# Moving the elementwise work between two layers from GpSimd to VectorE, and exchanging the places of three expert ranks

## The chip, the cores and the metric

The kernel runs on one core of a Trainium2 chip. The core has TensorE (PE in the profile; its weight loads are PEld), VectorE (DVE), ScalarE (ACT), GpSimd (POOL) and SyncE (SP), which here only issues loads. The metric is the device time of one execution in microseconds (us), median of several runs. The profile is that of one execution, and its times count from the start of its span.

## The reference, cut to what matters

Two layers work on 256 latent tokens and 256 context tokens of width 1024. Layer 0 is a recurrent block, layer 1 is attention with 16 query heads and 4 key heads. Behind each stands a mixture of 16 experts, of which every token takes two:

```python
for e in range(N_EXPERTS):
    y = y + gates[..., e:e + 1] * ((silu(h @ w1[e]) * (h @ w3[e])) @ w2[e])
ctx = ctx + cg_f * y[:, :C]          # layer 0: gain of the context
x = x + g_f * y[:, C:]               # layer 0: gain of the latent tokens
hx = modulate(x, ...); hc = modulate(ctx, ...)     # RMS norm, scale, shift
qx, kx, vx = split(hx @ qkv_w); kc, vc = split(hc @ qkv_w[:, q_cols:])
```

The stretch that the change works on is the end of layer 0's experts, the sum, the norm, and the projections of keys, values and queries.

## The kernel before, in words

**Experts of layer 0.** The 16 experts run in 16 slots, one after the other (`run`, lines 1166 to 1224). Slots 0 to 2 hold experts 0 to 2. The others are sorted by their number of tokens (rank 0 has the most), and `ORDERS` (line 38) says which rank stands in which slot: its 13 entries are slots 3 to 15. `ROOM` (line 39) gives each rank its rows: 192, 128, four times 96 (ranks 2 to 5), six times 64 (ranks 6 to 11), 32 (rank 12). `AGAIN` (line 41) lists the ranks that also have a second block of 128 rows under a run-time condition (rank 6 among them); such a slot costs branches on the engines in `ups`, `downs` and `fetch_next`, and its lists have two parts.

Each slot adds its result to the buffer `yr` in HBM by scatters that GpSimd issues (line 992), with accumulation. Each waits until the one before it has landed. A room of 64 or 32 rows takes one scatter, a room of 96 takes two (`BLOCKS`, line 63: a part of 64 rows and one of 32). Before the change the last three slots hold ranks 6, 5 and 12: one scatter, two, one. The weights of the experts are loaded by SP in a fixed order, 6 MB for each slot, into a ring of buffers.

**Between the experts and the attention** (`enter`, from line 1311). Weights and activations are split in two parts, `hi` (rounded) and `lo = w - hi`, and a product is three matmuls (`mm3`, line 180). The steps, in order of the code:

- `parts` (line 1337) splits one of the eight pieces of a weight: ScalarE copies to `hi`, and the engine given as `low` subtracts (line 1341). For the keys' and values' weights (`wkv`, line 1344) VectorE and GpSimd take turns; for the queries' weights (`wq`, line 1425) it is always GpSimd.
- `yr` is read back in four chunks of 128 tokens (line 1371), in the order 2, 3, 0, 1. Chunks 2 and 3 are latent tokens, 0 and 1 context.
- `gain(a)` (line 1377) multiplies a chunk with its gain: on VectorE for chunks 2 and 3, on GpSimd for 0 and 1. `add(a)` (line 1380) adds it to the residual on VectorE, and ScalarE squares and sums it. `modulated(a)` (line 1387) scales by the reciprocal root.
- `turn(a)` (line 1394) transposes a chunk on TensorE. For each of two halves it scales and shifts (VectorE for half 0, ScalarE for half 1, lines 1409 and 1407), rounds to `hhi` (VectorE, line 1411) and subtracts to `hlo` (line 1412): on VectorE for half 0, on GpSimd for half 1.
- `project_kv(a)` (line 1414) is a chunk's product with `wkv`; `project(n)` (line 1422) a half of the queries, with the splits of its weights; `keys` (line 1467), `norms` and `queries` are the norm and the rotation, on VectorE and ScalarE.

The block of lines 1509 to 1521 holds its own instructions in the written order on each engine, but the compiler's list scheduler may set instructions from outside it, such as the queries' splits, between them.

Of the kernel before, what the change touches and what calls it, by code (L numbers as in the profile page):

```python
# [34 lines left out]
ADA_AT = [32, 34]  # L35


ORDERS = [[11, 0, 10, 1, 9, 2, 8, 3, 7, 4, 6, 5, 12], [2, 0, 3, 1, 4, 5, 6, 7, 8, 9, 10, 11]]
ROOM = [[192, 128, 96, 96, 96, 96, 64, 64, 64, 64, 64, 64, 32], [160, 160, 32] + 9 * [32]]

AGAIN = [[1, 2, 3, 4, 6], [2, 3]]
# [25 lines left out]
def base(i, k):  # L67

    return BASE if k < FIRST[i] else ROOM[i][ORDERS[i][k - FIRST[i]]]


def again(i, k):

    return k < FIRST[i] or ORDERS[i][k - FIRST[i]] in AGAIN[i]


def room(i, k):
    return base(i, k) + 128 * again(i, k)
# [9 lines left out]
def hybrid_kernel(ctx: ExitStack, tc: tile.TileContext, x, c, ctxt, c_ctx, ada_w, ada_b, norm_mix_w, norm_ffn_w,  # L88
# [3 lines left out]
    nc = tc.nc  # L92
# [12 lines left out]
    def bank(name="bank"):  # L105
        if "spare" in banks:
            return banks["spare"]()
        return banks["pool"].tile([128, 512], F32, tag="bank", name=name)
# [61 lines left out]
    def take(key):  # L170
        return live[key][0]
# [394 lines left out]
    with tc.tile_pool(reuse_waits="tile", name="big0", bufs=1) as bp:  # L566
# [3 lines left out]
        hlo = hp.tile([128, NK, 512], F32R, name="hlo")  # L570
# [25 lines left out]
        with tc.tile_pool(reuse_waits="tile", name="n0", bufs=2) as n0, \  # L596
# [8 lines left out]
            hhi = wp.tile([128, 4096], F32R, tag="w", name="hhi").rearrange("p (k t) -> p k t", k=NK)  # L605
            parts = wp.tile([128, 4096], F32R, tag="w", name="parts")
# [704 lines left out]
    def enter(yr):  # L1311
# [6 lines left out]
        hlo = px.tile([128, 4096], F32R, tag="w", name="hlo1").rearrange("p (k t) -> p k t", k=NK)  # L1318
# [6 lines left out]
        def wide(name, dt=F32R):  # L1325
            return spare(name, dt).rearrange("p (k f) -> p k f", k=NK)

        wkv, wkvl, hhi = wide("wkv"), wide("wkvl"), wide("hhi")
        misc = spare("misc", F32)
        qd = [misc[:, 2048 + 1024 * z:3072 + 1024 * z].rearrange("p (h b f) -> p h b f", h=8, b=2) for z in range(2)]  # L1330
        gf = [misc[:, 2048 + 1024 * z:3072 + 1024 * z] for z in range(2)]
        n1 = ExitStack()
        yp = n1.enter_context(tc.tile_pool(reuse_waits="tile", name="n1", bufs=1))
        ys = [misc[:, 1024 * z:1024 * z + 1024] for z in range(2)] + [yp.tile([128, D], F32, name=f"y{z}") for z in (2, 3)]
        A, B = scale_vec(1, SC_M, 96, "am1"), vec(1, SH_M)

        def parts(key, hi, lo, k, low):

            w = take(key).rearrange("p (k f) -> p k f", k=NK)[:, k, :]
            nc.scalar.activation(hi[:, k, :], w, AF.Copy)  # L1340
            low.tensor_sub(lo[:, k, :], w, hi[:, k, :])

        for k in range(NK):
            parts(("qkv", 2), wkv, wkvl, k, (nc.vector, nc.gpsimd)[k % 2])
        region.close()
        pinned.__exit__(None, None, None)
        with tc.manual_schedule(engines={ET.PE, ET.Activation, ET.DVE, ET.Pool}):
# [27 lines left out]
        wq, wql = wide("wq"), wide("wql")  # L1375

        def gain(a):
            (nc.gpsimd, nc.vector)[a // 2].tensor_mul(ys[a], ys[a], gf[a // 2])

        def add(a):  # L1380
            nc.vector.tensor_add(xr[:, a, :], xr[:, a, :], ys[a])
            junk = ap.tile([128, D], BF16, tag="rtmp", name="junk", bufs=1)
            ss[a] = ap.tile([128, 1], F32, tag="ss", name="ss", bufs=4)
            nc.scalar.activation(junk, xr[:, a, :], AF.Square, accum_out=ss[a])
            nc.scalar.activation(ss[a], ss[a], AF.Sqrt, bias=eps, scale=1.0 / D)

        def modulated(a):
            nc.vector.reciprocal(ss[a], ss[a])
            if a < 2:
                nc.scalar.activation(ys[a], xr[:, a, :], AF.Copy, scale=ss[a])  # L1390
            else:
                nc.vector.tensor_scalar(ys[a], xr[:, a, :], ss[a], None, ALU.mult)

        def turn(a):
            j, ts = a // 2, slice(a * 128, a * 128 + 128)
            pbs = [bank(), bank()]
            for h in range(2):
                for k in range(4):
                    nc.tensor.transpose(pbs[h][:, k * 128:(k + 1) * 128], ys[a][:, (4 * h + k) * 128:(4 * h + k + 1) * 128],
                                        ident)  # L1400
            for h in range(2):
                m = yp.tile([128, 4, 128], F32, tag="m", name="m", bufs=2)
                for k in range(4):
                    kk = 4 * h + k
                    src = pbs[h][:, k * 128:(k + 1) * 128]
                    if h:
                        nc.scalar.activation(m[:, k, :], src, AF.Identity, bias=B[:, kk, j:j + 1], scale=A[:, kk, j:j + 1])
                    else:
                        nc.vector.tensor_scalar(m[:, k, :], src, A[:, kk, j:j + 1], B[:, kk, j:j + 1], ALU.mult, ALU.add)
                ks = slice(4 * h, 4 * h + 4)  # L1410
                nc.vector.tensor_copy(hhi[:, ks, ts], m)
                (nc.vector, nc.gpsimd)[h].tensor_sub(hlo[:, ks, ts], m, hhi[:, ks, ts])

        def project_kv(a, between=None):
            ts = slice(a * 128, a * 128 + 128)
            kvs[a] = pb = bank()
            for k in range(NK):
                if k == 4 and between is not None:
                    between()
                mm3(pb, hhi[:, k, ts], hlo[:, k, ts], wkv[:, k, :], wkvl[:, k, :], k == 0, k == NK - 1)  # L1420
# [88 lines left out]
        with tc.manual_schedule(engines={ET.PE, ET.Activation, ET.DVE, ET.Pool}):  # L1509
            gain(2)  # L1510
            add(2)
            gain(3)
            gain(0)
            gain(1)
            modulated(2)
            add(3)
            turn(2)
            modulated(3)
            project_kv(2, lambda: turn(3))
            for a in range(2):  # L1520
                add(a)
        project_kv(3)

# [13 lines left out]
        for a in range(2):  # L1537
            modulated(a)
            turn(a)
# [43 lines left out]
    class Heads:  # L1583
# [46 lines left out]
        def step(self, t):  # L1630
# [4 lines left out]
            if t >= 10 and t % 4 == 2:  # L1635
                self.weigh((t - 10) // 4)

    moe(R0, enter)
    with actx:
        heads = Heads()  # L1640
# [25 lines left out]
def _constants():  # L1666
# [30 lines left out]
    for i in range(2):  # L1697
        k = FIRST[i]
        a[:, C_KEY + 16 * i:C_KEY + 16 * i + 16] = np.where(x < k, 65536 + 16384 * (k - 1 - x), E - 1 - x)
        a[:, C_RANK + 16 * i:C_RANK + 16 * i + 16] = list(range(k)) + [k + r for r in ORDERS[i]]  # L1700
        a[:, C_ROOM + 16 * i:C_ROOM + 16 * i + 16] = [room(i, k) for k in range(E)]
# [32 lines left out]
```

## Time and profile before

| what | value |
|---|---|
| median of 3 runs | 992.27 us (991.25 to 992.55) |
| the profiled execution | 991.52 us, span 989.9 us |
| PE busy | 848.3 us (86% of the span) |
| DVE busy | 489.8 us (49%) |
| ACT busy | 302.8 us (31%) |
| POOL busy | 247.4 us (25%) |
| mean granted TensorE clock | 0.942 |

Shares over the whole span mix stages with different limits. Layer 0's experts run from about 317 to 595 us; the stretch from there to the first attention scores ends at about 675 us. In the timeline rows below the columns are start, duration (of a merged group of instructions), engine, line, operation, tiles, and in brackets how long the engine was idle before and what ended that. In rows of waits they are: the waiting engine, tile and line, what it waited for, us in total, times, the longest. In rows by source line: duration in ns (shortest, median, longest), first and last start.

### The profile page before, as it was taken

What the parts mean: (1) busy time and instruction counts of PE and PEld (TensorE: products, weight loads), DVE (VectorE), ACT (ScalarE), POOL (GpSimd) and SP (SyncE); (2) the same over time, 40 slices, a digit from 0 to 9 for tenths busy, and PEclk for the clock granted to TensorE, in tenths of its full rate; (3) what the DMA queues carried; (4) which work ended last, traced back from release to release, by engine and by line L of the source; (5) the groups of instructions that cost most, each with busy time, mean ns of one, the idle gap of its engine ahead of it and who ended that gap; (6) DMA issues with size and microseconds to landing.
All of it is one profiled execution on the core that took longest, in us unless ns stands there. A gap on an engine that the chain in (4) does not pass through costs nothing. (4 is left out here: it accounts for less than half of the span.)

```text
span 989.9 us, 17139 instructions
## 1 busy us (share of the span) xinstructions
PE 848.3 (86%) x6495; PEld 536.3 (54%) x6495; DVE 489.8 (49%) x1372; ACT 302.8 (31%) x555; POOL 247.4 (25%) x189
## 2 busy tenths in 40 slices
PE   3789899889996999999998963699999689799983
PEld 1356676575454655555555533487664555455652
DVE  2778797653147731312231115687861574523463
ACT  3546555674021211001010103556961220101110
POOL 2162233400002320211221115652430132312232
PEclk9899999998997999999999977799999799999997
DMA  9955974799525699999999994212939769999980
GB/s 346 358 183 200 388 262 170 259 386 383 205 83 214 215 360 384 371 356 362 355 342 365 376 338 133 102 58 77 388 125 393 272 234 373 376 388 361 376 270 10
DMA packets 126926, 277.11 MB, mean 280 GB/s; under 512 B 7673, under 2 KB 12889, under 8 KB 126816
## 3 DMA queue, kind: packets, MB, share of 16 engines
q1 hardware_dynamic: 116064, 253.77, 70.1%
q0 software_dynamic: 8880, 15.54, 6.7%
q10 hardware_dynamic: 1872, 6.37, 1.7%
q8 instruction: 64, 1.05, 0.4%
q14 instruction: 46, 0.38, 0.1%
HBM read 290.85 MB, written 14.81 MB: 309 GB/s over the span
## 5 line engine op out<-in xcount | busy, mean ns | idle before, releaser
L943 PE MATMUL up<-w,xg 128*64 128x256 f32 (+2 forms) x1888 | 173.8, 350 | 9.7 <-DMA w<-in_moe_w_dram 9.0
L943 PEld LDWEIGHTS up<-w,xg 128*64 128x64 f32 (+2 forms) x1888 | 108.6, 130 | 67.7 <-issue 32.2
L978 PE MATMUL py<-w,sx 128*32 128x256 f32 (+2 forms) x768 | 127.2, 513 | 5.9 <-DVE sx L957 4.0
L948 DVE TENSOR_TENSOR sx<-sx,up 128x256 f32<-128x256 f32 (+3 forms) x31 | 13.5, 434 | 186.5 <-PE up L943 108.9
L978 PEld LDWEIGHTS py<-w,sx 128*32 128x32 f32 (+2 forms) x768 | 44.8, 133 | 69.9 <-issue 52.8
L947 ACT ACTIVATE sx<-up 128x256 f32<-128x256 f32 (+3 forms) x31 | 12.2, 394 | 228.9 <-PE up L943 225.9
L582 POOL TENSOR_TENSOR parts<-w,parts 128x1024 fp32r<-128x1024 f32 x16 | 40.5, 2530 | 123.6 <-DVE parts L581 115.6
L992 POOL DMA_INDIRECT yr<-y,yi x21 | 32.8, 1564 | 122.0 <-DVE y L989 51.5
L528 PE MATMUL bank<-w,yT 128*128 128x512 f32 x128 | 57.3, 595 | 0.0
L182 PE MATMUL bank<-hhi,parts 128*128 128x512 f32 x128 | 52.3, 409 | 4.0 <-DVE parts L581 4.0
L184 PE MATMUL bank<-hhi,parts 128*128 128x512 f32 x128 | 51.5, 403 | 3.2 <-POOL parts L582 3.2
L183 PE MATMUL bank<-hlo,parts 128*128 128x512 f32 x128 | 52.3, 409 | 2.0 <-DVE hlo L397 1.9
L943 PE MATMUL up<-w,xr 128*32 128x128 f32 (+2 forms) x736 | 51.3, 315 | 2.9 <-issue 2.0
L915 POOL DMA_INDIRECT xg<-hr,gi x21 | 20.8, 990 | 124.0 <-DVE f L906 77.0
L316 PE MATMUL bank<-w,st 128*32 128x512 f32 x384 | 46.5, 615 | 3.5 <-DMA w<-in_ada_w_dram 3.1
L943 PEld LDWEIGHTS up<-w,xr 128*32 128x32 f32 (+2 forms) x736 | 35.5, 120 | 16.0 <-issue 10.5
L930 ACT ACTIVATE xg<-tp 128x512 f32<-128x512 f32 x32 | 17.4, 594 | 84.3 <-PE tp L925 71.8
L989 DVE TENSOR_SCALAR y<-py,gt 128x512 f32<-128x512 f32 (+1 forms) x21 | 14.4, 687 | 56.6 <-PE py L978 54.9
L462 DVE TENSOR_TENSOR rt<-bank,gm 128x512 f32<-128x512 f32 x12 | 8.3, 691 | 66.9 <-PE bank L528 66.9
L528 PEld LDWEIGHTS bank<-w,yT 128*128 128x128 f32 x128 | 23.4, 190 | 25.7 <-issue 25.5
L1607 POOL TENSOR_SCALAR pe<-pe,mx 128x512 f32<-128x512 f32 x16 | 25.0, 1567 | 45.3 <-DVE mx L1602 30.0
L992 POOL DMA_INDIRECT out_dram<-xr,yi x14 | 22.1, 1581 | 50.9 <-DVEq L1163 11.9
(358 smaller groups left out, 1624.6 us busy)
## 6 DMA issues: line engine op xcount, KB each, us to landing
w<-in_moe_w_dram SPq DMA_DIRECT2D x192, 1024.0 KB
w<-in_ada_w_dram SPq DMA_DIRECT2D x48, 1024.0 KB
w<-in_lru_in_w_dram SPq DMA_DIRECT2D x8, 1024.0 KB
w<-in_attn_qkv_w_dram SPq DMA_DIRECT2D x6, 1024.0 KB
w<-in_lru_out_w_dram SPq DMA_DIRECT2D x4, 1024.0 KB
w<-in_attn_o_w_dram SPq DMA_DIRECT2D x4, 1024.0 KB
hr<-h ACTq DMA_DIRECT2D x6, 512.0 KB
yr<-zero POOLq DMA_DIRECT2D x4, 512.0 KB
```

The costliest lines, as they stand in the source:

```text
L182: nc.tensor.matmul(pb, wh, xh, start=start, stop=False, skip_group_check=True)
L183: nc.tensor.matmul(pb, wh, xl, start=False, stop=False, skip_group_check=True)
L184: nc.tensor.matmul(pb, wl, xh, start=False, stop=stop, skip_group_check=True)
L316: nc.tensor.matmul(pa[32 * g:32 * g + 32, :], st[:, 4 * r + g, :], w[:, 4 * r + g, :], start=r == 0, stop=r == 1, skip_group_check=True, t ...
L528: nc.tensor.matmul(pb, src[:, k, n * 128:(n + 1) * 128], w[:, k, :], start=k == 0, stop=k == NK - 1)
L582: nc.gpsimd.tensor_sub(lo, w, h)
L915: nc.gpsimd.indirect_dma_start(out=dst[0:rows, :], out_offset=None, in_=hr[:, :], in_offset=bass.IndirectOffsetOnAxis(ap=idx[0:rows, :], a ...
L930: nc.scalar.activation(dst, pb, AF.Copy)
L943: nc.tensor.matmul(pw[g * Tn:(g + 1) * Tn, at:at + fg], hT[:, k, t0:t0 + Tn], W[:, k, g * fg:(g + 1) * fg], start=k == 0, stop=k == NK - 1 ...
L978: nc.tensor.matmul(py[j * Tn:(j + 1) * Tn, 0:wd], aT[:, ao + q * 128 + g * Tn:ao + q * 128 + (g + 1) * Tn], W2[:, f, j * dg + h * 512:j * ...
L992: nc.gpsimd.indirect_dma_start(out=yr[:, :].rearrange("r (g f) -> (r g) f", g=G), out_offset=bass.IndirectOffsetOnAxis(ap=ls.yi[:, z, b:b ...
L1607: (nc.gpsimd if u else nc.vector).tensor_scalar(pe, pe, mx[:, 1:2], None, ALU.mult)
```

## The change

The keys' and values' weights are split by VectorE alone; all four gains and all lower halves of the activations are computed by VectorE. The gains of chunks 0 and 1 now come right before their additions. GpSimd keeps its scatters, gathers and the queries' splits. In layer 0, slot 3 gets rank 6 (was 11), slot 13 rank 5 (was 6), slot 14 rank 11 (was 5).

```diff
-ORDERS = [[11, 0, 10, 1, 9, 2, 8, 3, 7, 4, 6, 5, 12], [2, 0, 3, 1, 4, 5, 6, 7, 8, 9, 10, 11]]
+ORDERS = [[6, 0, 10, 1, 9, 2, 8, 3, 7, 4, 5, 11, 12], [2, 0, 3, 1, 4, 5, 6, 7, 8, 9, 10, 11]]
...
         for k in range(NK):
-            parts(("qkv", 2), wkv, wkvl, k, (nc.vector, nc.gpsimd)[k % 2])
+            parts(("qkv", 2), wkv, wkvl, k, nc.vector)
...
         def gain(a):
-            (nc.gpsimd, nc.vector)[a // 2].tensor_mul(ys[a], ys[a], gf[a // 2])
+            nc.vector.tensor_mul(ys[a], ys[a], gf[a // 2])
...
                 nc.vector.tensor_copy(hhi[:, ks, ts], m)
-                (nc.vector, nc.gpsimd)[h].tensor_sub(hlo[:, ks, ts], m, hhi[:, ks, ts])
+                nc.vector.tensor_sub(hlo[:, ks, ts], m, hhi[:, ks, ts])
...
             gain(3)
-            gain(0)
-            gain(1)
             modulated(2)
...
             for a in range(2):
+                gain(a)
                 add(a)
```

## Rows read from the trace of the kernel before

**Rows 1.** Windows of three stretches: us, busy time by engine, PEclk, DMA share, GB/s
```profile
560.00:586.00 26.00, 18.83 (x257) 10.39 (x255) 2.21 (x5) 1.44 (x4) 3.10 (x2) 0.84 1.04 376
...
643.00:655.90 12.90, 12.90 (x66) 10.74 (x65) 10.20 (x23) 6.51 (x16) 5.62 (x4) 1.00 0.19 73
655.90:671.00 15.10, 13.89 (x69) 11.33 (x68) 13.46 (x29) 7.60 (x18) 8.22 (x7) 1.00 0.33 119
```

**Rows 2.** Waits from 596 to 672 us
```profile
PE bank L1399 <- DVE y L1392: 12.4, 1, 12.4
...
PE bank L184 <- POOL hlo L1412: 5.2, 1, 5.2
...
PE bank L1504 <- DVE misc L1498: 1.2, 1, 1.2
DVE m L1409 <- POOL hlo L1412: 1.2, 1, 1.2
```

**Rows 3.** Timeline of POOL from 561 to 640 us
```profile
561.50 1.55 POOL L992 DMA_INDIRECT yr<-y,yi  x1 [7.73 <-issue]
570.82 1.55 POOL L992 DMA_INDIRECT yr<-y,yi  x1 [7.77 <-DVEq L1163]
590.10 1.55 POOL L992 DMA_INDIRECT yr<-y,yi  x1 [17.73 <-DVE y L989]
596.99 1.55 POOL L992 DMA_INDIRECT yr<-y,yi  x1 [5.33 <-issue]
600.77 1.55 POOL L992 DMA_INDIRECT yr<-y,yi  x1 [2.23 <-DMA yr<-y,yi]
...
613.35 5.93 POOL L1378 TENSOR_TENSOR misc<-misc 128x1024 f32<-128x1024 f32 x2 [1.24 <-DMA misc<-yr]
...
625.05 13.21 POOL L1341 TENSOR_TENSOR wql<-w,wq 128x512 fp32r<-128x512 f32 x8
638.23 1.26 POOL L1412 TENSOR_TENSOR hlo<-m,hhi 128x512 fp32r<-128x512 f32 x1
```

**Rows 4.** Timeline of DVE from 609 to 671 us
```profile
609.51 1.47 DVE L1378 TENSOR_TENSOR y<-y,misc 128x1024 f32<-128x1024 f32 x1 [4.61 <-DMA y<-yr]
611.02 2.17 DVE L1381 TENSOR_TENSOR xr<-xr,y 128x1024 f32<-128x1024 f32 x1
...
614.93 2.14 DVE L1392 TENSOR_SCALAR y<-xr,ss 128x1024 f32<-128x1024 f32 x1
617.00 3.37 DVE L1381 TENSOR_TENSOR xr<-xr,y 128x1024 f32<-128x1024 f32 x1
...
629.61 1.67 DVE L1412 TENSOR_TENSOR hlo<-m,hhi 128x512 fp32r<-128x512 f32 x1
...
632.63 4.51 DVE L1381 TENSOR_TENSOR xr<-xr,misc 128x1024 f32<-128x1024 f32 x2
...
639.58 0.16 DVE L1388 RECIPROCAL ss<-ss 128x1 f32<-128x1 f32 x1 [2.04 <-ACT ss L1385]
643.87 0.42 DVE L1444 TENSOR_REDUCE hss<-sq 128x4 f32<-128x256 f32 x1 [4.12 <-ACT sq L1443]
```

**Rows 5.** Source lines 371, 1341 and 1378: durations in ns
```profile
L371 DVE TENSOR_SCALAR xn<-xr,ss x4: 746/750/754, 19.3 to 22.5; 128x1024 f32<-128x1024 f32 x4
...
L1341 DVE TENSOR_TENSOR wkvl<-w,wkv x4: 677/677/694, 600.0 to 602.6; 128x512 fp32r<-128x512 f32 x4
...
L1341 POOL TENSOR_TENSOR wkvl<-w,wkv x4: 1255/1255/2241, 606.2 to 609.9; 128x512 fp32r<-128x512 f32 x4
...
L1378 DVE TENSOR_TENSOR y<-y,misc x2: 1212/1342/1473, 609.5 to 613.1; 128x1024 f32<-128x1024 f32 x2
```

**Rows 6.** Waits of PE, from 346 to 534 us (two rows) and from 534 to 600
```profile
PE tp L925 <- PEq L1147: 1.6, 5, 0.3
PE pa L955 <- PEq L1163: 1.6, 4, 0.6
...
PE up L943 <- DMA w<-in_moe_w_dram: 9.0, 6, 2.8
```

## The prediction

> **What bounds the kernel now.** I read the windows first, then the waits, then GpSimd's and VectorE's timelines, because the change only moves work between engines and places.
>
> Layer 0's experts end under the load of their weights: from 560 to 586 us the DMA engines' share is 1.04 at 376 GB/s, while TensorE is busy 18.83 of 26 us [rows 1], and from 534 to 600 us it waits six times, 9.0 us in all, for those weights [rows 6]. When the last weight arrives is therefore no matter of slots; what counts there is the tail behind it. The reader is to see that tail in GpSimd's timeline: scatters at 590.10, 596.99 and 600.77, each one waiting until the one before has landed, and VectorE's first gain at 609.51, when the sum has come back from HBM [rows 3, 4].
>
> From 609.5 to 671 us TensorE is short of work. It waits 12.4 us for the first normed chunk, 5.2 us for a `hlo` of GpSimd and 1.2 us for the queries of VectorE [rows 2]. The 5.2 us are a queue, not work: that subtraction takes 1.26 us, but at 638.23, since eight splits of the queries' weights went before it from 625.05, for 13.21 us [rows 3]. What feeds TensorE the rest of the time is VectorE, busy 10.20 of 12.9 us and 13.46 of 15.1 us in the last two windows [rows 1].
>
> **How the two engines disturb each other.** The second `add` starts at 617.00 and takes 3.37 us; GpSimd's two gains end at 613.35 + 5.93 = 619.28, and the remaining 1.09 us are about what a VectorE instruction of this size with two inputs takes by itself, 1.21 us [rows 3 to 5]. So it stood still until GpSimd had finished and then ran at full speed. The scaling at 614.93 took 2.14 us beside the same two gains, and 0.75 us in a calm place [rows 4, 5]. I price by this: alone 1.21 us (1024 columns, two inputs), 0.68 us (512), 0.75 us (scaling of 1024); next to GpSimd's splits up to 1.67 us for 512 columns [rows 4, 5].
>
> **The change part by part.**
>
> *Ranks.* Slot 14 has one scatter in place of two. The scatter at 590.10 stays, for its result waits for VectorE and the weights, and the next at 596.99 is then the last slot's: 600.77 - 596.99 = 3.8 us earlier, and with it all that reads the sum. Slot 13 now has two scatters. In full DMA traffic they follow each other by 570.82 - 561.50 = 9.3 us [rows 3]; two from 570.82 are over at 589.4, 0.7 us before 590.10, so they just fit. If they don't, slot 14's is late by as much as they miss; the ends are 0 and -3.8, and I take -3.8, since the spacing is measured under the heaviest load. The wider slot 13 has more TensorE work and slot 14 as much less, under the 9.0 us of waiting for weights [rows 6]. Slot 3 gets the condition: slots that have it show 1.6/5 = 0.3 us and 1.6/4 = 0.4 us on TensorE [rows 6], in a stretch whose end the weights set. Were that cover gone, it would cost 0.7 us; I take 0. Also its lists have a second part, a few short VectorE instructions under the same cover.
>
> *Splits of the keys' and values' weights.* Four more on VectorE, 4 x 0.68 = 2.7 us [rows 5], behind its four from 600.0 to 603.3. The sum is read back 3.8 us earlier, at 605.7 in place of 609.5, so VectorE, which was idle for 4.61 us there [rows 4], ends at about 605.9. Cost 0.2 us. GpSimd's four, of 1.26 to 2.24 us, go [rows 5].
>
> *First chunks.* GpSimd has nothing to do until the queries' weights have come. VectorE's chain loses the standstills: gain 1.47 to 1.21, `add` 2.17 to 1.21, scaling 2.14 to 0.75, `add` 3.37 to 1.21, together 9.15 - 4.38 = 4.8 us [rows 4, 5]. With the ranks that is -8.6, less 0.2: -8.4 us at the first rounding of `hhi`, and TensorE's first wait shrinks as much.
>
> *Second half of the chunks.* TensorE's wait of 5.2 us goes. What is late next is VectorE: on its queue before the second context chunk's norm there are now two `hlo` (2 x 1.67 = 3.3 us at the price next to the splits) and two gains (2.4; they stop nobody, for the context's sums were read back by 613.35 [rows 3]), while the two `add` fall from 4.51 to 2.4 us, as the splits are over by then, having also started earlier. Its second `add`, over at 632.63 + 4.51 = 637.14, moves by -8.4 + 3.3 + 2.4 - 2.1 = -4.8, to 632.3. From there to the norm's reciprocal at 639.58 it was 2.4 us, which gives 634.7 and then the keys. Before, the keys began at 643.87, after 4.12 us in which VectorE waited for the product that the late `hlo` had held up [rows 4]; that product is now over before VectorE is free. So the keys start 9.1 us earlier. The standstills that I left out (an instruction between two splits may stand for up to one split, 1.26 us [rows 5]) give some back: I take -8.2, between -7 and -9.5.
>
> *Behind that* VectorE has two more `hlo` (2 x 0.68 = 1.4 us) and no longer waits 1.2 us for GpSimd [rows 2]: +0.2. TensorE, which gained more, then waits for VectorE's queries longer than the 1.2 us of before. The stretch ends 8.0 us earlier. From there on nothing is changed, and all loads of layer 1 follow the attention's buffers; the whole shift reaches the end.
>
> The sum: 989.9 - 8.0 = 981.9 us of span, 983.5 us for the profiled execution (1.6 us lie around the span); the median of the runs is 0.75 us above that execution, so 984.3 us.
>
> Work that VectorE takes over can also hurt the scatters. In the trace, the scatter at 600.77 has VectorE's splits beside it and takes 1.55 us, as do the four before it [rows 3, 5]. [...]
>
> **The rivals.**
> - *TensorE, not VectorE, sets the end.* Then the shift is 3.8 + 4.8 + 5.2 = 13.8 less a little idle clock, some -12: 980.3 us. For it: the 5.2 us wait is TensorE's own. Against: VectorE's windows are nearly full and get four instructions more. Chance 0.11.
> - *The scatters don't get shorter*, because slot 13's second one is late and pushes slot 14's. Then only -4.2 remain: 988.1 us. The margin was 0.7 us. Chance 0.14.
> - *Slower: VectorE is the bound all the way, and its standstills don't go*, because the queries' splits, with nothing before them on GpSimd, start as early as the first chain and lie beside all of it. Then the added work costs four `hlo` at 1.67 and two gains at the longest standstill seen, 3.37: 13.4 us. Saved are the 4.1 and 1.2 us that VectorE waited and the scatters' 3.8: +4.3, 996.6 us. It decides if splits begin before the second `add`. Against: before, they began 15.5 us after the first gain [rows 3, 4]. Chance 0.06.
> - *VectorE's eight splits hold the last scatter back*, 8 x 0.68 = 5.4 us: 989.7 us. Against: it is issued at 597, three us before the first split. Chance 0.04.
> - *Nothing measurable*: the compiler places the moved subtractions behind other VectorE work and TensorE's wait only changes its name; around 992. Chance 0.06.
>
> **How the numbers follow.** The forecast has 0.59: 984.3 us, with -6 to -9.5 around it. The range reaches to the first rival below and the fourth above: 980 to 989.5. A measurement of this kernel can tell 0.2%, 2.0 us, from no change. Faster by more: 0.59 + 0.11 + 0.14 + most of the fourth, 0.88; within it 0.06; slower 0.06.
>
> **What would show it.** Right: two scatters after 590, 3.8 us earlier at the end; the first chain of VectorE at 1.2, 1.2, 0.75 and 1.2 us; no wait of TensorE for GpSimd; a longer wait for VectorE's queries. Wrong: slot 14's scatter after 591; GpSimd's splits before 615; keys that start later than 637.

## The result and the profile after

The changed kernel takes 982.73 us (median of 4 runs, 980.47 to 984.45) against 992.41 us (median of 4 runs): ratio 0.991, 95% interval 0.9893 to 0.9927. A second measurement beside the last experiments gave 0.9913, interval 0.989 to 0.9936. The forecast was 984.3 us.

| what | after |
|---|---|
| the profiled execution | 980.47 us, span 978.8 us |
| PE busy | 848.3 us (87% of the span) |
| DVE busy | 490.8 us (50%) |
| POOL busy | 229.7 us (23%) |

The profiled executions of the two kernels are already 3.0 us apart where nothing was changed: slot 0's first product starts at 324.40 us before and at 321.40 after. So I measure stages from there. *Experts* runs from slot 0's first product to VectorE's first gain, *front* from that gain to the first attention score on TensorE, *rest* from there to the end of the span.

| us | start of slot 0 | first gain | first score | experts | front | rest |
|---|---|---|---|---|---|---|
| before | 324.40 | 609.51 | 675.59 | 285.1 | 66.1 | 314.3 |
| after | 321.40 | 602.21 | 662.95 | 280.8 | 60.7 | 315.9 |
| after, second profile | 324.74 | 606.39 | 666.08 | 281.6 | 59.7 | 315.6 |

Experts and front together are 9.6 us shorter in one profile and 9.9 us in the other. The rest is unchanged code; over the profiles of all kernels below it lies between 314.0 and 318.9 us, so its differences here say nothing of the change.

GpSimd's timeline after (start, duration, line, tiles, idle time before and what ended it):

```profile
570.33 1.55 POOL L992 DMA_INDIRECT yr<-y,yi  x1 [6.29 <-DVE sx L957]
579.18 1.55 POOL L992 DMA_INDIRECT yr<-y,yi  x1 [7.30 <-DMA yr<-y,yi]
587.00 1.55 POOL L992 DMA_INDIRECT yr<-y,yi  x1 [6.26 <-DMA yr<-y,yi]
593.50 1.55 POOL L992 DMA_INDIRECT yr<-y,yi  x1 [4.95 <-DMA yr<-y,yi]
612.73 11.68 POOL L1341 TENSOR_TENSOR wql<-w,wq 128x512 fp32r<-128x512 f32 x8 [17.68 <-ACT wq L1340]
634.16 7.12 POOL L1341 TENSOR_TENSOR wql<-w,wq 128x512 fp32r<-128x512 f32 x5 [9.76 <-ACT wq L1340]
```

Two scatters stand at the end where three stood [rows 3]: slot 14's at 587.00 and slot 15's at 593.50. Counted from slot 0, slot 14's starts at 265.6 us and the last at 272.1; before they were at 265.7 and 276.4. Slot 13's two, at 570.33 and 579.18, lie before them. Then GpSimd is idle for 17.68 us until the queries' weights come.

VectorE's timeline after, the same columns, from the splits of the keys' and values' weights to the keys:

```profile
593.99 4.89 DVE L1341 TENSOR_TENSOR wkvl<-w,wkv 128x512 fp32r<-128x512 f32 x8
...
602.21 1.22 DVE L1378 TENSOR_TENSOR y<-y,misc 128x1024 f32<-128x1024 f32 x1 [2.56 <-DMA y<-yr]
603.47 1.22 DVE L1381 TENSOR_TENSOR xr<-xr,y 128x1024 f32<-128x1024 f32 x1
...
606.43 0.75 DVE L1392 TENSOR_SCALAR y<-xr,ss 128x1024 f32<-128x1024 f32 x1
607.10 1.22 DVE L1381 TENSOR_TENSOR xr<-xr,y 128x1024 f32<-128x1024 f32 x1
...
609.79 0.43 DVE L1411 CAST hhi<-m 128x512 fp32r<-128x512 f32 x1
...
611.72 0.69 DVE L1412 TENSOR_TENSOR hlo<-m,hhi 128x512 fp32r<-128x512 f32 x1
...
616.36 1.37 DVE L1409 TENSOR_SCALAR m<-bank,am,adT 128x128 f32<-128x128 f32 x4 [3.09 <-PE bank L1399]
...
618.47 1.67 DVE L1412 TENSOR_TENSOR hlo<-m,hhi 128x512 fp32r<-128x512 f32 x1
...
621.60 1.66 DVE L1412 TENSOR_TENSOR hlo<-m,hhi 128x512 fp32r<-128x512 f32 x1
623.18 2.31 DVE L1378 TENSOR_TENSOR misc<-misc 128x1024 f32<-128x1024 f32 x1
...
626.87 1.22 DVE L1378 TENSOR_TENSOR misc<-misc 128x1024 f32<-128x1024 f32 x1
628.12 1.23 DVE L1381 TENSOR_TENSOR xr<-xr,misc 128x1024 f32<-128x1024 f32 x1
...
629.34 0.40 DVE L1444 TENSOR_REDUCE hss<-sq 128x4 f32<-128x256 f32 x1
...
630.94 0.16 DVE L1388 RECIPROCAL ss<-ss 128x1 f32<-128x1 f32 x1
631.06 0.42 DVE L1473 TENSOR_TENSOR kn<-bank,hss 128x256 f32<-128x256 f32 x1
...
638.48 1.67 DVE L1412 TENSOR_TENSOR hlo<-m,hhi 128x512 fp32r<-128x512 f32 x1
...
641.81 0.68 DVE L1412 TENSOR_TENSOR hlo<-m,hhi 128x512 fp32r<-128x512 f32 x1
...
644.46 2.39 DVE L1412 TENSOR_TENSOR hlo<-m,hhi 128x512 fp32r<-128x512 f32 x2
```

The first chain runs at 1.22, 1.22, 0.75 and 1.22 us, where it took 1.47, 2.17, 2.14 and 3.37 us [rows 4]. Where GpSimd's splits lie beside it (612.73 to 624.4, and again from 634.16), a `hlo` still takes 1.67 us.

TensorE's waits after, from 590 to 665 us (tile and line, what it waited for, us, times, longest):

```profile
PE bank L1399 <- DVE y L1392: 9.0, 1, 9.0
...
PE bank L1504 <- DVE misc L1498: 2.8, 1, 2.8
PE bank L1399 <- ACT misc L1390: 1.5, 1, 1.5
```

The 5.2 us for GpSimd's `hlo` [rows 2] are gone, and no wait of TensorE for GpSimd is left. The wait for VectorE's queries grew from 1.2 to 2.8 us.

### The profile page after: what moved, and what is told of

Read it like the earlier page. It is cut to its first block, busy times and chain, and to the rows that moved or that the text cites. A ratio compares the mean times of both kernels' runs of the same rounds, so it can differ in the third digit from the quotient of the medians.

```text
span 978.8 us, 17130 instructions
## 1 busy us (share of the span) xinstructions
PE 848.3 (87%) x6495; PEld 538.9 (55%) x6495; DVE 490.8 (50%) x1382; ACT 302.2 (31%) x555; POOL 229.7 (23%) x179
## 5 line engine op out<-in xcount | busy, mean ns | idle before, releaser
L978 PE MATMUL py<-w,sx 128*32 128x256 f32 (+2 forms) x768 | 125.1, 507 | 7.4 <-DVE sx L957 3.7
```

The costliest lines, as they stand in the source:

```text
L978: nc.tensor.matmul(py[j * Tn:(j + 1) * Tn, 0:wd], aT[:, ao + q * 128 + g * Tn:ao + q * 128 + (g + 1) * Tn], W2[:, f, j * dg + h * 512:j * ...
```

## The experiments

Each edit is shown against the kernel before, where nothing else is said. In "experts" and "front" the stages above are meant; those of before are 285.1 and 66.1 us.

**The ranks alone.**

```diff
-ORDERS = [[11, 0, 10, 1, 9, 2, 8, 3, 7, 4, 6, 5, 12], ...
+ORDERS = [[6, 0, 10, 1, 9, 2, 8, 3, 7, 4, 5, 11, 12], ...
```

> The kernel before with the new ranks alone. Measures: the experts' stretch, from the first up matmul of slot 0 to the first gain (285.1 us before, 280.8 after), and the attention's front, from the first gain to the first score matmul (66.1 before, 60.7 after). If the two halves of the change are separate, the experts' stretch is 280.8 here, the front stays at 66.1, and the time is 4.3 us under before, ratio about 0.996. Rival: the tail is shorter but the front gives it back (GpSimd's splits are then earlier beside the first chunks): ratio 1.000.

Measured: ratio 0.9959 (0.9939 to 0.9979), experts 282.7, front 66.3 us. The time is as expected, but the experts' stretch of this profile is 1.9 us longer than expected. A row of GpSimd's timeline shows the reason for part of it:

```profile
590.79 1.55 POOL L992 DMA_INDIRECT yr<-y,yi  x1 [5.60 <-DMA yr<-y,yi]
```

This is slot 14's scatter. VectorE had its result ready at 588.69, but slot 13's second scatter, begun at 583.63, had to land first. So it starts 267.8 us after slot 0, 2.1 us later than before, and the last one 3.0 us earlier than before.

**The moved work alone.** All of the diff but its `ORDERS` line.

> The change without the ranks. If the halves are separate, the experts' stretch is 285.1, the front 60.7, and the time 5.3 us under before, ratio 0.9945. Rival: the engines' half is all of it, ratio 0.991, and the ranks bring nothing.

Measured: ratio 0.995 (0.9931 to 0.9968), experts 284.9, front 60.5 us. Each half of the change shortens its own stage, by 2.4 and 5.6 us, and leaves the other nearly as it was; the two gains in time, 0.41% and 0.50%, add up to the whole 0.9%.

**The lower halves of the activations alone.**

```diff
-                (nc.vector, nc.gpsimd)[h].tensor_sub(hlo[:, ks, ts], m, hhi[:, ks, ts])
+                nc.vector.tensor_sub(hlo[:, ks, ts], m, hhi[:, ks, ts])
```

> The kernel before with only the lower half of the activations moved to VectorE. TensorE's wait of 5.2 us for GpSimd must go in either theory. If VectorE sets the pace of the front (forecast), most of it comes back as a wait for VectorE: the front is 64 to 65.5 us, 0.7 to 2.4 less than before, ratio 0.998 to 0.999. If TensorE's wait was time by itself (rival), the front is 61 us and the ratio 0.995.

Measured: ratio 0.9992 (0.9972 to 1.0012), front 66.3 us. TensorE's waits in this kernel, from 590 to 675 us:

```profile
PE bank L1399 <- DVE y L1392: 14.3, 1, 14.3
PE bank L1504 <- DVE misc L1498: 4.1, 2, 2.8
```

and two instructions of its VectorE timeline, each of which is two subtractions:

```profile
650.10 2.38 DVE L1412 TENSOR_TENSOR hlo<-m,hhi 128x512 fp32r<-128x512 f32 x2
...
654.48 2.39 DVE L1412 TENSOR_TENSOR hlo<-m,hhi 128x512 fp32r<-128x512 f32 x2
```

The wait of 5.2 us for GpSimd is gone and nothing was gained. Counted from the first gain, the keys do start earlier, at 31.7 in place of 34.4 us (639.40 - 607.74, 643.87 - 609.51). Behind them VectorE now has four `hlo` in place of two, 4.8 us in place of 2.35, and TensorE waits 4.1 us for the queries. Of the 5.2 us, VectorE gives back 2.3: TensorE begins the last transposes of the queries 59.2 us after the first gain, before 61.5. The front is not shorter even so, because of what follows. From these transposes to the first score, in the columns of [rows 1], before and in this kernel:

```profile
671.01:675.59 4.58, 4.58 (x29) 3.89 (x29) 2.09 (x6) 4.29 (x10) 0.00 (x0) 1.00 0.19 70
...
666.98:674.06 7.08, 7.08 (x28) 6.04 (x29) 2.08 (x6) 4.39 (x10) 0.00 (x0) 0.60 0.00 1
```

TensorE does the same work there without a pause. Before, it had waited 1.2 us just ahead of it and ran at a granted clock of 1.00, its upper level of 2.4 GHz. Here it had waited 2.8 us, and the clock was 0.50 (1.2 GHz) from 666.9 to 669.4 us and 0.60 on the mean, which took 2.5 us more. So the 5.2 us of waiting went in two ways: VectorE's queue kept more than half, and TensorE's clock, behind a longer wait for VectorE, took the rest. This is one profile; how often the clock falls in the other eleven runs is not known.

**The gains alone**, on VectorE and right before their additions.

```diff
-            (nc.gpsimd, nc.vector)[a // 2].tensor_mul(ys[a], ys[a], gf[a // 2])
+            nc.vector.tensor_mul(ys[a], ys[a], gf[a // 2])
...
-            gain(0)
-            gain(1)
...
             for a in range(2):
+                gain(a)
                 add(a)
```

> The kernel before with only the gains of the two context chunks moved to VectorE and next to their additions. Forecast: the scaling of the first chunk falls from 2.14 to 0.75 us and the second add from 3.37 to 1.21, the late lower half stays behind the queries' splits but all of it comes 3.5 us earlier, so the front is 62.6 us and the ratio 0.9965. Rival: the two gains cost VectorE as much later as the standstills cost before, front 66, ratio 1.000.

Measured: ratio 0.9965 (0.9946 to 0.9984), front 63.8 us. The time was as expected, the front 1.2 us longer than expected; TensorE now waits 6.2 us for GpSimd's `hlo` in place of 5.2. The gains alone leave that subtraction in its queue, where it now holds TensorE up longer, and the two gains, beside the queries' splits, take 2.31 and 2.28 us on VectorE.

**The splits of the keys' and values' weights alone.**

```diff
-            parts(("qkv", 2), wkv, wkvl, k, (nc.vector, nc.gpsimd)[k % 2])
+            parts(("qkv", 2), wkv, wkvl, k, nc.vector)
```

> The kernel before with only the four odd splits of the keys' and values' weights moved to VectorE. Forecast: they lie in VectorE's idle time before the sum is read back; the first gain and the first add lose their standstills (1.47 and 2.17 to 1.21 us each), so the front is 1.2 us shorter, 64.9 us, ratio 0.999. Rival (VectorE's splits starve the last scatter): the experts' stretch grows by up to 5.4 us.

Measured: ratio 0.9989 (0.9975 to 1.0003), experts 286.7, front 65.5 us: not told from no change. The first gain and the first `add` take 1.23 and 1.22 us, as expected. Of the 1.6 us by which the experts' stretch is longer, 1.3 lie ahead of the last scatter, which itself takes 1.77 us, so the rival shows with some 0.2 us at most.

Singly the three moves give 0.08%, 0.35% and 0.11%, in sum 0.54%, and together 0.50%. With some 0.2% of uncertainty on each, the times do not say whether the moves help one another. The fronts hint at it, +0.2, -2.3 and -0.6 us against -5.6 together, but each is one profile; this stays open.

**The changed kernel with its gains in the old place**, all four on VectorE (against the kernel after):

```diff
             gain(3)
+            gain(0)
+            gain(1)
...
             for a in range(2):
-                gain(a)
                 add(a)
```

> The changed kernel with the two context gains on VectorE, but in their old place before the first chunk's scaling. They put 2.4 us on the path to TensorE's first matmul and take 2.4 us off VectorE's queue later. If VectorE's whole queue is what bounds the front, the time is that of the changed kernel within 1 us (0.991 of before); if the way to TensorE's first product is, it is 2.4 us slower (0.9935).

Measured: ratio 0.9932 (0.9909 to 0.9955), front 63.0 us, 2.3 us more than the changed kernel's 60.7. The intervals of the two times overlap a little. A row of its VectorE timeline:

```profile
608.24 2.35 DVE L1378 TENSOR_TENSOR misc<-misc 128x1024 f32<-128x1024 f32 x2
```

The two gains stand ahead of the first scaling, and TensorE's first product waits for them: it starts 9.9 us after the first gain, in the changed kernel 8.2. But VectorE has made that up by the end of the context's second `add`, 25.8 us after the first gain against 27.1 and 27.5 in the two profiles of the changed kernel. It loses time after that:

```profile
633.16 0.16 DVE L1388 RECIPROCAL ss<-ss 128x1 f32<-128x1 f32 x1 [2.10 <-ACT ss L1385]
633.43 0.42 DVE L1444 TENSOR_REDUCE hss<-sq 128x4 f32<-128x256 f32 x1
```

In this kernel the compiler put the second context chunk's reciprocal, which waits 2.10 us for ScalarE, ahead of the keys' second sum; in the changed kernel it stands behind it (629.34 and 630.94). So the sum starts 28.7 us after the first gain in place of 27.1 and 27.5. Behind it, TensorE's clock takes part again: 6.70 us at 0.65 from the last transposes of the queries to the first score, in the changed kernel 5.98 and 4.57. The time comes out as expected of the second case, but what these rows show is the order in VectorE's queue and the clock, and not only the way to TensorE's first product.

**The changed kernel with the context's gains on GpSimd**, in the new place (against the kernel after):

```diff
-            nc.vector.tensor_mul(ys[a], ys[a], gf[a // 2])
+            (nc.gpsimd, nc.vector)[a // 2].tensor_mul(ys[a], ys[a], gf[a // 2])
```

> The changed kernel with the two context gains back on GpSimd, but in the new place, so that engine and place come apart. GpSimd's own time for one is about 2.3 us. If they sit behind the queries' splits in its queue, the context chunks come later and TensorE waits for them: 3 to 6 us slower than the changed kernel (0.994 to 0.997 of before). If place alone mattered, it is as fast as the changed kernel, or faster by the 2.4 us that VectorE is spared.

Measured: ratio 0.996 (0.9944 to 0.9976), 0.5% above the changed kernel's 0.991; front 64.5 us, 3.8 more. This is within what was expected, but not for the reason given: the gains do not sit behind the queries' splits, which start at 617.49. GpSimd's timeline, one row, and VectorE's, two:

```profile
607.81 5.09 POOL L1378 TENSOR_TENSOR misc<-misc 128x1024 f32<-128x1024 f32 x2 [11.73 <-ACT ss L1385]
```

```profile
607.97 2.73 DVE L1392 TENSOR_SCALAR y<-xr,ss 128x1024 f32<-128x1024 f32 x1
610.61 3.37 DVE L1381 TENSOR_TENSOR xr<-xr,y 128x1024 f32<-128x1024 f32 x1
```

The standstill of the kernel before is back to the hundredth: the `add` takes 3.37 us and ends at 613.98, 1.08 us after GpSimd's gains end at 607.81 + 5.09 = 612.90. Before, it was 1.09 us. GpSimd's gains lie beside the first chain in both orders. The Trainium skill (SBUF — State Buffer, SBUF: two separate sides) calls the port pair that the two engines share an exclusive lock: of a GpSimd instruction that reads SBUF and a VectorE one with two inputs there, whichever starts first keeps it for the whole instruction. Both pairs of rows agree. The chain is 4.0 us later at its first `hhi`, but only 1.0 us at the end of the context's second `add`; then this kernel, too, has the reciprocal that waits 2.10 us for ScalarE ahead of the keys' second sum. How much of the 3.8 us is that order, and how much the standstills, was not tried apart.

**Two single scatters ahead of the last.** The changed kernel left slot 14's result waiting: VectorE had it ready at 584.03 + 0.75 us, and its scatter went out at 587.00, behind slot 13's second one. So I put rank 5, with two scatters, further ahead (against the kernel after):

```diff
-ORDERS = [[6, 0, 10, 1, 9, 2, 8, 3, 7, 4, 5, 11, 12], ...
+ORDERS = [[6, 0, 10, 1, 9, 2, 8, 3, 5, 4, 7, 11, 12], ...
```

> The changed kernel with the ranks once more exchanged, so that slots 13 and 14 both take one scatter and the rank with two stands in slot 11. In the changed kernel slot 14's scatter waited for slot 13's second one, from 585.0 (its result ready) to 587.0. If that wait is on the path, the tail is 2.0 us shorter and the time 2.0 us under the changed kernel, some 0.989 of before. If other scatters queue up instead, or the read-back is bound by the weights' loads, it is the same as the changed kernel, 0.991.

Measured: ratio 0.9942 (0.9922 to 0.9962), experts 284.1 us. A miss: no gain, but this stage is 2.4 to 3.3 us longer than in the two profiles of the changed kernel. The last scatter starts only some 0.2 us earlier, counted from slot 0, than in the changed kernel's first profile. In the second one, taken later, the wait that this run was to remove is hardly there: slot 14's scatter goes out 0.3 us after its result. GpSimd's last scatter and, beside it, VectorE's splits:

```profile
595.98 5.23 POOL L992 DMA_INDIRECT yr<-y,yi  x1 [6.55 <-DVE wkvl L1341]
```

```profile
594.72 4.89 DVE L1341 TENSOR_TENSOR wkvl<-w,wkv 128x512 fp32r<-128x512 f32 x8
```

The scatter ends at 601.21, 1.60 us after the splits' end at 599.61, and its usual time is 1.55 us: it looks as if it had to wait for VectorE to be through. Four runs followed on this.

*VectorE has four of the eight splits* (the line of `parts` as before, the rest as the last kernel):

> Ranks 5 and 6 and the moved work as in the kernel with two single scatters, but VectorE and GpSimd take turns again with the eight splits of the keys' and values' weights, so that VectorE has four of them, not in one streak, and GpSimd's four lie behind its last scatter. If VectorE's streak of eight stretched the last scatter from 1.55 to 5.23 us: the last scatter takes 1.6 to 2 us, the experts' stretch (first product of slot 0 to first gain) falls from 284.1 to 280.5 to 281.5 us, the front may lose up to 1 us to GpSimd's splits, and the ratio is 0.990 to 0.992. If the length was that of this scatter for another reason (its place, its rows, its queue): it stays at 5.2 us, the stretch at 284, the ratio at 0.994 to 0.995.

Measured: ratio 0.9902 (0.9877 to 0.9926), experts 282.3, front 60.2 us; last scatter 2.06 us.

*VectorE does each split twice* (the last kernel, with one line more in `parts`):

```diff
             low.tensor_sub(lo[:, k, :], w, hi[:, k, :])
+            if low is nc.vector:
+                low.tensor_sub(lo[:, k, :], w, hi[:, k, :])
```

> As the kernel with two single scatters, but each of the eight splits of the keys' and values' weights is done twice on VectorE, one behind the other, so that its work there takes some 10 us in place of 4.9. If GpSimd can't issue the scatter while VectorE works through the splits: the last scatter, begun at about 596, lasts until VectorE is through, 9 to 10 us in place of 5.23, the first gain comes 4 to 5 us later, and the ratio is 0.998 to 1.000. If the scatter's length has nothing to do with the splits: it stays at 5.2 us (or falls to 1.55), the splits lie in VectorE's idle time before the first gain, and the ratio stays at 0.994 to 0.995.

Measured: ratio 0.9922 (0.9899 to 0.9944), experts 281.1, front 62.9 us. A miss: with twice the work on VectorE the last scatter is short.

```profile
592.61 1.75 POOL L992 DMA_INDIRECT yr<-y,yi  x1 [5.45 <-DVE rope L1363]
```

It was no longer quite the same case, though: the compiler set some of the rotation's short instructions between the splits, five of the sixteen stand behind the first gain, and the scatter began 0.49 us after the first split (592.12), in place of 1.26.

*The changed kernel once more, beside these two:*

> The changed kernel as it is, once more on the chip of the two runs beside it: 0.9893 to 0.9927 as measured before, last scatter 1.55 us, stretch of the experts 280.8 us, front 60.7 us. If it comes out at 0.993 or above, part of the lag of the kernel with two single scatters behind it was that of its chip.

Measured: ratio 0.9913 (0.989 to 0.9936), experts 281.6, front 59.7 us, last scatter 1.55 us.

*The kernel with two single scatters once more:*

> The kernel with two single scatters once more, unchanged, because doubling VectorE's splits did not lengthen the last scatter (1.75 us). If the 5.23 us belong to this order of instructions: the last scatter takes about 5 us again, the experts' stretch 284 us, and the ratio is 0.994. If they were an accident of that one profiled execution: 1.6 to 2 us, a stretch of 281 to 282 us, and a ratio of 0.990 to 0.992, as the changed kernel.

Measured: ratio 0.9944 (0.993 to 0.9959), experts 283.7, front 60.9 us. The same again: GpSimd's last scatter and VectorE's splits.

```profile
593.96 5.61 POOL L992 DMA_INDIRECT yr<-y,yi  x1 [6.55 <-DVE wkvl L1341]
```

```profile
593.07 4.89 DVE L1341 TENSOR_TENSOR wkvl<-w,wkv 128x512 fp32r<-128x512 f32 x8
```

It ends at 599.57, 1.61 us after the splits (597.96). So the long scatter belongs to this order of instructions and is no accident of one execution. But eight splits of VectorE in a row are not enough to make it. In the kernel with the moved work alone the scatter lies in the middle of such a row:

```profile
598.15 1.72 POOL L992 DMA_INDIRECT yr<-y,yi  x1 [2.23 <-DVE wkvl L1341]
```

```profile
596.54 4.90 DVE L1341 TENSOR_TENSOR wkvl<-w,wkv 128x512 fp32r<-128x512 f32 x8 [1.51 <-issue]
```

What decides whether it gets through stays open. The rows that differ: in the two long cases ScalarE's copies of the same weights still run beside it (the second four from 595.64 to 597.83), and the scatter before it lies 8.1 us back, against 3.8 here. Neither was tried by itself.

The version with four splits on each engine is the fastest median (981.79 us, against 982.86 for the changed kernel in the same measurement), but the intervals of the two lie almost wholly on each other: no version was shown to beat the changed kernel.

## Why the prediction was right, step by step

Positions are counted from slot 0's first product, so that the 3.0 us ahead of it drop out; the two values are those of the two profiles of the changed kernel.

| step | forecast, us | measured, us |
|---|---|---|
| last scatter | -3.8 | -4.3, -4.4 |
| first gain | -3.6 | -4.3, -3.5 |
| first chain, gain to first `hhi` (12.17 before) | -4.8 | -4.6, -4.6 |
| context's second `add` ends (312.74 before) | -4.8 | -4.8, -3.6 |
| keys' sums start (319.47 before) | -8.2 | -11.5, -10.3 |
| from there to the first score (31.72 before) | +0.2 | +1.9, +0.5 |
| the whole stretch | -8.0 | -9.6, -9.9 |

**Ranks: right, though the margin was thinner than one profile shows.** In the changed kernel slot 14's scatter stays where it was (265.6 and 265.4 us after slot 0, 265.7 before) and the last one follows it by 6.5 and 6.6 us in place of 10.7. The ranks alone give 0.9959, and 0.996 would be -3.8 us. The second rival's cause, that slot 13's second scatter pushes slot 14's, did come true: in the ranks alone by 2.1 us. In the first profile of the changed kernel slot 14's scatter waited 2.2 us for it as well, but its result was ready about as much earlier, and in the second it waited 0.3 us. The forecast had the two scatters of slot 13 just fit, by 0.7 us; that they cost the changed kernel nothing is in part luck. The prediction also says of all three scatters of before that they waited for the one ahead to land; the first of them, at 590.10, waited for VectorE's result.

**Splits of the keys' and values' weights: right** that they cost next to nothing; by themselves they give 0.9989 with 1.0 in the interval.

**First chain: right**, 4.6 us of the forecast 4.8, and for the reason given: the kernel with the gains back on GpSimd brings the second `add`'s standstill back with the same length, and the scaling's with 2.73 in place of 2.14 us.

**Second half: the sum right up to the `add`, then one size off.** VectorE's queue moved the second `add` by 4.8 and 3.6 us, 4.8 as worked out, but the parts of that sum offset each other: the two added `hlo` took 0.69 and 1.66 us in place of 2 x 1.67, the two gains 2.31 and 1.22 in place of 2.4 together, and VectorE waited 3.09 us for TensorE's transposes of the second chunk, 1.50 before, which the sum does not have. The step that failed is "From there to the norm's reciprocal at 639.58 it was 2.4 us, which gives 634.7 and then the keys". The keys' sums did not wait for that reciprocal: they start as the `add` ends (629.34), and the reciprocal, at 630.94, comes after them. That is 2.4 us more than the sum of 9.1 in the first profile, and with the second 2.1 to 3.3 more than the -8.2 that I took.

**Behind the keys' sums: VectorE's part right, TensorE's clock left out.** Two `hlo` more were priced at 2 x 0.68 us, as if GpSimd's splits were over. They are not: five of them run from 634.16 for 7.12 us, and the four `hlo` there take 1.67, 0.68 and 2.39 us, together 4.74 in place of 2.35. Two steps of the keys' rotation, now without splits beside them, took 0.62 and 0.63 us in place of 2.83 and 1.73. Up to TensorE's last transposes of the queries it is +0.5 us in both profiles, +0.2 forecast. The rest of the first profile's +1.9 lies behind that, where the two profiles of the same kernel differ:

```profile
656.97:662.95 5.98, 5.98 (x29) 5.27 (x29) 2.08 (x6) 4.40 (x10) 0.00 (x0) 0.73 0.02 4
...
661.51:666.08 4.57, 4.57 (x28) 3.88 (x29) 2.09 (x6) 4.29 (x10) 0.00 (x0) 1.00 0.01 2
```

In both TensorE had just waited 2.8 us for the queries; in the first its clock then fell, in the second it did not, which is 1.4 us. The forecast saw the longer wait coming and put nothing on what follows it.

Together, 1.6 to 1.9 us are left by which the stretch is shorter than forecast. The second profile's span, 981.7 us, is close to the forecast 981.9 all the same, because its unchanged rest took 1.3 us more than before: that is luck.

**VectorE, not TensorE, sets the pace: right for most of the front.** Taking the 5.2 us wait away by itself brought TensorE's last transposes only 2.3 us forward, and TensorE waits longer for the queries, as forecast. But VectorE's own place in the sum depends on waits of 3.09 us for TensorE and, in some of the kernels, of 2.10 us for ScalarE, and the last stretch is TensorE's. The first rival, with TensorE as the bound, had -12 us: the measured -9.7 lies between it and the forecast of -8.0.

**The other rivals.** The slower one, with the queries' splits beside the first chain, did not happen: they start at 612.73, 10.5 us after the first gain and behind the second `add` (608.32). The sign that I gave for it, splits before 615, is met in this profile all the same; it should have been told from the first gain, not by the clock time. The fourth, VectorE's splits that hold back the last scatter, is not in the changed kernel (1.55 us in both profiles). The reason that I gave against it did not hold, though: the splits came forward with the scatter and began 0.5 and 2.2 us after it, not three. Two profiles with another order of ranks show a long scatter, 3.7 to 4.1 us longer where the price was 5.4.

## What to carry to other kernels

When an engine's wait is to be removed, first ask which queue its next value comes from, and what the engine does after the wait that replaces it: here 5.2 us of TensorE's waiting were worth nothing by themselves, because VectorE's queue gave back less than half and TensorE then ran at half its clock for a while. Elementwise work on GpSimd next to a critical chain of VectorE can cost that chain as much as doing the work there: the two gains take 3.5 us on VectorE behind its first chain in the changed kernel, and moving them alone freed that chain of 3.4 us and the front of 2.3. When two versions differ in one moved line, compare the order of all instructions on the engine: the compiler may have moved others too. Where serial scatters end a stage, put the slot that needs fewest of them last, and look in the profile at what the neighbour engine does while the last one is issued.

## What was not expected of the hardware

A scatter that GpSimd issues beside VectorE's two-input subtractions can take 5.23 and 5.61 us in place of 1.55, ending one usual scatter's time after them. In seven other kernels, the one before among them, a last scatter that began after the first of such subtractions took 1.55 to 2.06 us. The Trainium skill (SBUF — State Buffer, Who interferes with whom) says that a copy on VectorE was seen to stall DMAs of GpSimd, and that two-input instructions were not. The short scatters agree with it; the two long ones do not, if it was the subtractions that held them, which the two equal ends suggest and no run shows. The run with sixteen subtractions was to decide and could not, since its instructions came in another order.

TensorE's clock can fall behind a wait at the end of the front. In the ten profiles in which TensorE waited 2.8 us for the queries, the granted clock of the stretch up to the first score was 0.60 to 0.74 in seven, and the stretch took 5.9 to 7.1 us; in the other three it was 1.00 and 4.57 us. In the four in which it waited 0.4 to 1.3 us there, the clock was 1.00 each time. What decides between the seven and the three was not tried.
